# Conditioning weights requested between the output-projection loads on one queue, and one burst's transposes issued after the next burst

## The chip, the cores and the metric

The kernel runs on one core of a Trainium2 chip. The metric is the device time of one execution in microseconds (us). Engines are named as the profile names them: PE is the matrix engine (PEld its weight loads), DVE the vector engine, ACT the scalar engine, POOL the GpSimd engine, SP the sync engine. SP and POOL issue DMAs here, each on a queue of its own (q1 and q0 in the profile).

## The reference, cut to what matters

A decoder layer runs on 320 tokens: 256 of a prompt and 8 samples of 8 tokens. Every weight is shared. A conditioning vector per sequence makes six modulation vectors; the two last of them (`sc2`/`sh2` for the second norm, `g2` for the second residual) are used behind the mixing part:

```python
mod = jax.nn.silu(c) @ w_ada + b_ada
sh1, sc1, g1, sh2, sc2, g2 = [m[:, None, :] for m in jnp.split(mod, 6, axis=-1)]
...
merged = jax.nn.sigmoid(ga) * y_a + jax.nn.sigmoid(gb) * y_b
x = x + g1 * (merged @ w_o)

h2 = _rmsnorm(x, norm2_g) * (1 + sc2) + sh2
gate, up = jnp.split(h2 @ w_gu, 2, axis=-1)
x = x + g2 * ((jax.nn.silu(gate) * up) @ w_down)
```

`D_MODEL` is 2048, so `w_ada` is 2048 x 12288, `w_o` 2048 x 2048, `w_gu` 2048 x 11264, all float32.

## The kernel before, in words

Activations lie with channels on the 128 partitions and the 320 tokens along the free axis. Each float32 weight is split into a high and a low part of a shorter type (`whi` by ACT at L151, `wlo` by DVE at L152), each activation likewise, and a product is three matmuls (L165, L166, L167). A projection (`proj`, L169) takes 256 output columns at a time. It reads its weight in *chunks* of 512 rows x 256 columns (0.5 MB, one DMA on SP at L143, buffer `raw` with three slots), splits each chunk in two halves of two row blocks (`whi` and `wlo` have four slots), and gives 24 matmuls for each chunk (four row blocks, two column blocks, three products).

The output projection `w_o` is eight such units of four chunks (loop at L979), 32 chunks in all; this text counts them from 0 to 31, so that chunk `4*ui + c//4` is the one that `between(c - k0)` (L180) follows. `between` is `x1_rows` (L970), which at a unit's first chunk asks on SP for two 160 KB blocks of the saved residual stream (L975). After each unit `residual` and `sq_acc` update the residual stream and the sum of squares on DVE and ACT, and POOL makes `xs` (L985).

Beside this, `mod` is computed in *bursts* (`BURSTS`, L245): a burst multiplies 4 or 8 row blocks of `w_ada` (1024 columns wide) on PE, in four column strips at once (`ada_burst`, L273, matmuls at L284). Its weights lie in `araw`, are listed by `ada_load` (L262), and are requested piece by piece by `ada_piece` (L254) on POOL's queue. When the last burst of a column range is done, ACT copies the sums (`adasb`, L291), PE transposes them twice (L293, recorded as L129) and DVE adds the bias into `mod` (L296); this part is called the closing here.

Bursts 0 to 23 are loaded and run earlier. Bursts 24 and 25 (eight row blocks each; together the first half of `g2`) and burst 26 (four row blocks; the first quarter of the second half) are listed at L977 and requested during `w_o`: after each of the two POOL operations at L985 of a unit, one piece of two row blocks (1 MB), so ten pieces in all. They run right behind `w_o`: burst 24, the matmul that sums the squares over the partitions (`rstd_bcast`, L991), burst 25 with its closing, burst 26. Then `h2` is made (L1006 to L1015) and the gate and up projections (`w_gu`) begin, the first two side by side (`projs`, L183), their matmuls issued behind the last matmul of burst 26 (`issue_after`, L1082).

The order of each engine's instructions is set when the program is built: a planner takes the program order as priority and simulates when each instruction becomes ready. `issue_after(x)` adds that an instruction stands behind `x` in its engine's order. Each engine and each queue then works strictly in that order. Pools that are closed (`mix` and `acx`, L944 and L945) give their memory to the pools opened behind them, among them `aw` (L949), which holds `xs`, `araw` and `adasb` for bursts 24 to 26.

Of the kernel before, what the change touches and what calls it, by code (L numbers as in the profile page):

```python
# [15 lines left out]
ALU = mybir.AluOpType  # L16
# [4 lines left out]
P = 128  # L21
TP, NB, LS = 256, 8, 8
TS = NB * LS
T = TP + TS
# [58 lines left out]
def body(tc, A):  # L83
    nc = tc.nc
# [12 lines left out]
    def nm(s):  # L97
        uid[0] += 1
        return "%s_%d" % (s, uid[0])

    def misc():
        return pmisc.tile([P, 512], F32, tag="m", name=nm("pm"))

    V, S, G, PE = nc.vector, nc.scalar, nc.gpsimd, nc.tensor
# [22 lines left out]
    def tr(out, in_):  # L127
        k = in_.shape[0]
        PE.transpose(out, in_, ident[:k, :k])  # L129
# [3 lines left out]
    last_raw = []  # L133
# [35 lines left out]
    def proj(w, col, k0, k1, xh, xl, between=None):  # L169

        ps = pmain.tile([P, 2, 512], F32, tag="pm", name=nm("ps"))
        for c0 in range(k0, k1, 4):
            nk = min(4, k1 - c0)
            for j, whi, wlo in split_chunk(w[:, c0:c0 + nk, col:col + 256], nk, 256):
                kt = c0 + j
                for i in range(2):
                    mm3(ps[:, i, :T], whi[:, i * P:(i + 1) * P], wlo[:, i * P:(i + 1) * P],
                        xh[kt], xl[kt], kt == k0, kt == k1 - 1)
            if between:
                between(c0 - k0)  # L180
        return ps
# [26 lines left out]
    wada = A["w_ada"][0].rearrange("(kt p) n -> p kt n", p=P)  # L208
# [35 lines left out]
    NBA = 8  # L244
# [5 lines left out]
    ada_want = []  # L250
# [2 lines left out]

    def ada_piece(after=None):  # L254

        n, t, r = ada_want.pop(0)
        sec, b, k0, nk = BURSTS[n]
        col = (sec * KT + b) * P
        with tc.issue_after(after) if after is not None else nullcontext():
            nc.gpsimd.dma_start(t[:, r:r + 2], wada[:, k0 + r:k0 + r + 2, col:col + NBA * P])  # L260

    def ada_load(n, bufs):  # L262

        if n < len(BURSTS) and n not in ada_raw:
            nk = BURSTS[n][3]
            t = ada_raw[n] = apool[0].tile([P, nk, NBA * P], F32, tag="big" if nk == 4 else "big2", bufs=bufs if nk == 8 else 1, name=nm("araw"))
            ada_want.extend((n, t, r) for r in range(0, nk, 2))

    def ada_all():
        while ada_want:  # L270
            ada_piece()

    def ada_burst():  # L273

        n = len(ada_done)
        sec, b, k0, nk = BURSTS[n]
        ada_done.append(n)
        if k0 == 0:
            ada_ps[:] = [misc()]
        ps = ada_ps[0]  # L280
        with tc.high_priority(), tc.issue_after(last_mm[0]):
            for r in range(nk):
                for j in range(4):
                    last_ada[:] = [PE.matmul(ps[32 * j:32 * j + 32, 0:2 * P], lhsT=scT[:, k0 + r, :],  # L284
                                             rhs=ada_raw[n][:, r, 2 * j * P:(2 * j + 2) * P],
                                             start=k0 + r == 0, stop=k0 + r == KT - 1, tile_position=(0, 32 * j)).ins]
        if k0 + nk < KT:
            return
        pt = misc()
        sb = apool[0].tile([P, 2 * P], F32, tag="adasb", name=nm("adasb"))  # L290
        S.copy(sb, ps[:, 0:2 * P])  # L291
        for q in range(2):
            tr(pt[:, q * P:(q + 1) * P], sb[:, q * P:(q + 1) * P])  # L293
        blk = slice(sec * KT + b, sec * KT + b + NBA)
        bb = bada[:, blk].rearrange("p (j q) -> p j q", q=2).unsqueeze(3).broadcast_to([P, 4, 2, 9])
        V.tensor_tensor(mod[:, blk, :].rearrange("p (j q) r -> p j q r", q=2),  # L296
                        pt[:, 0:2 * P].rearrange("p (q j r) -> p j q r", q=2, j=4)[:, :, :, 0:9], bb, op=ALU.add)
        if sec == 4:
            V.tensor_tensor(mod[:, blk, :], mod[:, blk, :],
                            N2G[:, b:b + NBA].unsqueeze(2).broadcast_to([P, NBA, 9]), op=ALU.mult)  # L300
# [4 lines left out]
    def mods(sec, kt):  # L305
        return mod[:, sec * KT + kt, 1:9].unsqueeze(2).broadcast_to([P, NB, LS])

    def s3(ap):
        return ap.rearrange("p (b t) -> p b t", t=LS)
# [87 lines left out]
    with tc.tile_pool(name="head", bufs=1) as xp:  # L397
# [43 lines left out]
        for i in range(3):  # L441
            n = P if i < 2 else TS
# [469 lines left out]
    RATE = 10  # L912
    BURST_UNITS = (0, 1, 2, 3, 7, 8, 9, 10)
    ada_load(0, 1)
    ada_all()
    for h in range(1, H):
        pump(RATE)
        g = new_group(h)
        for ui, (kind, i, col) in enumerate(units(h)):
            if kind == "og" and i == 0:  # L920
                pump(len(queue))
                new_gates(g)
            ps = proj(win, col, 0, KT, hh, hl)
            evac(ps, g, kind, i, None)
            if kind == "u":
                pump(len(queue))
                st, E = gla_steps(g)
                pst, psy = pool_steps(g)
                queue += pst + st
            if ui in BURST_UNITS:  # L930
                ada_burst()
                if len(ada_done) < AMIX:
                    ada_load(len(ada_done), 1)
                    ada_all()
            pump(RATE)
        queue += psy + [merge_step(g, E)]
# [13 lines left out]
    x1 = [fp.tile([P, T], F32, name="x1_%d" % k) for k in range(KT)]  # L950
    acc = fp.tile([P, T], F32, tag="acc", name="acc1")

    def sq_acc(acc, k, first):
        if first:
            S.activation(acc, x1[k], AF.Square)
        else:
            sq = fp.tile([P, T], F32, tag="sq", bufs=2, name=nm("sq"))
            S.activation(sq, x1[k], AF.Square)
            V.tensor_tensor(acc, acc, sq, op=ALU.add)

    def residual(ps, i, k, sec):
        V.scalar_tensor_tensor(x1[k][:, 0:TP], ps[:, i, 0:TP], modp(sec, k), x1[k][:, 0:TP],
                               op0=ALU.mult, op1=ALU.add)
        t = fp.tile([P, TS], F32, tag="rt", bufs=2, name=nm("rt"))
        V.tensor_tensor(s3(t), s3(ps[:, i, TP:T]), mods(sec, k), op=ALU.mult)
        V.tensor_tensor(x1[k][:, TP:T], x1[k][:, TP:T], t, op=ALU.add)

    xs = apool[0].tile([P, KT, TS], F32, name="xs")
    tiny = fp.tile([P, 1], F32, name="tiny")
    def x1_rows(c):  # L970

        if c == 0:
            with tc.issue_after(last_raw[0]):
                for k in (2 * ui, 2 * ui + 1):
                    nc.sync.dma_start(x1[k], xspill[k])  # L975

    for n in range(AMIX, AMIX + 3):  # L977
        ada_load(n, 2)
    for ui in range(8):  # L979
        ps = proj(wo, 256 * ui, 0, KT, mh, ml, between=x1_rows)  # L980
        for i in range(2):
            residual(ps, i, 2 * ui + i, 2)
            k = 2 * ui + i
            sq_acc(acc, k, k == 0)
            gi = G.tensor_tensor(s3(xs[:, k]), s3(x1[k][:, TP:T]), mods(4, k), op=ALU.mult).ins  # L985
            if ada_want:
                ada_piece(gi)
        if ui == 6:
            S.activation(tiny, epst, AF.Sqrt)

    def rstd_bcast(acc):  # L991
        pt = misc()
        last_mm[:] = [PE.matmul(pt[:, 0:T], lhsT=ones, rhs=acc, start=True, stop=True).ins]
        rs = fp.tile([P, T], F32, tag="rs", name=nm("rs"))
        S.activation(rs, pt[:, 0:T], AF.Sqrt, scale=1.0 / D, bias=epst)
        V.reciprocal(rs, rs)
        return rs

    more[:] = [fa, None]
    ada_burst()  # L1000
    rs = rstd_bcast(acc)
    ada_burst()
    ada_burst()
    h2h = [hp.tile([P, T], F32R, tag="hh%d" % k, name="h2h%d" % k) for k in range(KT)]
    h2l = [hp.tile([P, T], F32R, tag="hl%d" % k, name="h2l%d" % k) for k in range(KT)]
    for k in range(KT):  # L1006
        t = apool[0].tile([P, T], F32, tag="h2", bufs=3, name=nm("h2"))
# [69 lines left out]
    for pi, (f0, f1) in enumerate(parts):  # L1077
# [37 lines left out]
        for ui in range(8):  # L1115
            if pi == 1 and ui == 7:
                break
            ps = proj(wdn, 256 * ui, f0, f1, ah, al)
            for i in range(2):
                k = 2 * ui + i  # L1120
# [7 lines left out]
    ps = pmain.tile([P, 2, 512], F32, tag="pm", name=nm("ps"))  # L1128
# [3 lines left out]
    for c0 in range(f0, f1, 4):  # L1132
        nk = min(4, f1 - c0)
        raw = raw_chunk(wdn[:, c0:c0 + nk, 256 * 7:256 * 8], nk, 256)
        for j in range(0, nk, 2):
            q = c0 - f0 + j
# [14 lines left out]
    with tc.manual_schedule(engines={mybir.EngineType.PE}):  # L1151
        for kt in range(f0, f1):
            PE.matmul(pb, lhsT=ahl[kt], rhs=whl[kt][0], start=kt == f0, stop=False)
            PE.matmul(pb, lhsT=ahl[kt], rhs=whl[kt][1], start=False, stop=kt == f1 - 1)
            if kt in (f0 + 7, f0 + 10):
                i = 0 if kt == f0 + 7 else 1
                k = KT - 2 + i
# [9 lines left out]
    for i in range(2):  # L1167
        k = KT - 2 + i
        t = fp.tile([P, TS], F32, tag="rt", bufs=2, name=nm("rt"))
# [26 lines left out]
```

## Time and profile before

| | us |
|---|---|
| median of three runs | 1974.52 |
| lowest, highest | 1974.08, 1975.68 |
| the profiled execution: its own time | 1972.61 |
| the profiled execution: its span | 1970.7 |
| busy PE / DVE / ACT / POOL in the span | 1927.2 / 1003.3 / 822.3 / 204.7 |

The span is the time between the first and the last recorded instruction; about 1.9 us of the execution lie outside it. The busy share of PE counts overlapping matmuls and their modelled ends, so small gaps are seen better from the start times of single matmuls in the timeline. In a timeline row stand the start, the duration (from the first to the last of the merged instructions), the engine, the line, what is written and read, the count, and in brackets how long the engine had been idle and what released it. In the view by stretches each row has the stretch, its length, the busy time and count of each engine, the granted clock, the share of the DMA engines and GB/s.

The stage of `w_o` runs from about 880 to 1006 us of the span, and the change lies between 911 and 1018 us.

### The profile page before, as it was taken

The page shows a single profiled execution, that of the slowest core. Times are in us where ns is not written, and L with a number is a line of the kernel's source. Part 1 is how long each engine was busy: PE and PEld are TensorE (multiplying, and loading weights), DVE is VectorE, ACT ScalarE, POOL GpSimd, SP SyncE. Part 2 cuts the span into 40 slices and gives each one's busy share as a digit, 9 for nine tenths or more (in the row PEclk, how much of TensorE's full clock was granted, in tenths as well). Part 3 has the DMA queues.
Part 4 walks back from the last instruction along what each step waited for, and adds up shares of the span by engine and source line. Part 5 has one row for each costly group of instructions (what it writes and reads, how often), then busy time and mean ns, then how long its engine had stood idle before and what let it go on. Part 6 is the DMA issues. An engine that isn't in the chain of part 4 may idle for free.

```text
span 1970.7 us, 34879 instructions
## 1 busy us (share of the span) xinstructions
PE 1927.2 (98%) x13900; PEld 1811.9 (92%) x13900; DVE 1003.3 (51%) x1894; ACT 822.3 (42%) x1472; POOL 204.7 (10%) x352
## 2 busy tenths in 40 slices
PE   5999999999999999999999999999999999999998
PEld 3778988988899889988989999999999999999998
DVE  2655655655356535665474444444444444444554
ACT  3323553643345433553344333433333434344444
POOL 1002211221122112111130000000000000000000
PEclk9999999999999999999999999999999999999999
DMA  9995558758865787479935554444444444444443
GB/s 339 340 338 181 189 174 292 246 192 312 279 218 168 267 292 261 129 254 326 320 114 194 191 184 142 149 153 144 157 146 152 149 152 150 150 148 149 140 150 107
DMA packets 310206, 400.95 MB, mean 203 GB/s; under 512 B 12898, under 2 KB 273858, under 8 KB 309706
## 3 DMA queue, kind: packets, MB, share of 16 engines
q1 hardware_dynamic: 279914, 291.17, 45.8%
q0 software_dynamic: 30128, 107.55, 14.8%
q8 instruction: 109, 1.79, 0.4%
q14 instruction: 55, 0.44, 0.1%
HBM read 374.23 MB, written 24.67 MB: 202 GB/s over the span
## 4 chain that ended last, share of the span: by engine, by line
PE 82%; DMA 2%; ACT 1%; DVE 1%; issue 0%; POOL 0%; ACTq 0%; DVEq 0%; POOLq 0%
PE ps L167 25%; PE ps L165 25%; PE ps L166 25%; PE pm L284 3%; PE pm L129 1%; DMA araw<-w_ada 1%; PE pm L779 1%; PE pm L758 1%; DMA raw<-w_o 1%; PE pm L723 1%; DMA raw<-w_in 1%; PE pm L712 0%; DVE wlo L152 0%; PE pm L653 0%; ACT whi L151 0%
## 5 line engine op out<-in xcount | busy, mean ns | idle before, releaser
L152 DVE TENSOR_TENSOR wlo<-raw,whi 128x512 fp32r<-128x512 f32 x941 | 648.9, 694 | 773.6 <-ACT whi L151 760.7
L151 ACT CAST whi<-raw 128x512 fp32r<-128x512 f32 x941 | 579.2, 621 | 899.9 <-PE ps L166 802.2
L165 PE MATMUL ps<-hh,whi 128*128 128x320 f32 x1408 | 441.8, 314 | 3.1 <-ACT whi L151 2.1
L167 PE MATMUL ps<-hh,wlo 128*128 128x320 f32 x1408 | 436.0, 312 | 2.0 <-DVE wlo L152 1.9
L166 PE MATMUL ps<-hl,whi 128*128 128x320 f32 x1408 | 436.4, 310 | 0.0
L165 PE MATMUL ps<-h2h,whi 128*128 128x320 f32 x1408 | 434.6, 309 | 0.0
L166 PE MATMUL ps<-h2l,whi 128*128 128x320 f32 x1408 | 434.3, 309 | 0.0
L167 PE MATMUL ps<-h2h,wlo 128*128 128x320 f32 x1408 | 434.2, 309 | 0.0
L165 PEld LDWEIGHTS ps<-hh,whi 128*128 128x128 f32 x1408 | 264.5, 188 | 27.6 <-issue 16.1
L167 PEld LDWEIGHTS ps<-hh,wlo 128*128 128x128 f32 x1408 | 263.7, 188 | 17.5 <-issue 9.5
L166 PEld LDWEIGHTS ps<-hl,whi 128*128 128x128 f32 x1408 | 264.7, 188 | 4.3 <-issue 3.2
L165 PEld LDWEIGHTS ps<-h2h,whi 128*128 128x128 f32 x1408 | 264.5, 188 | 1.2 <-ACT ah L315 1.2
L166 PEld LDWEIGHTS ps<-h2l,whi 128*128 128x128 f32 x1408 | 264.5, 188 | 0.0
L167 PEld LDWEIGHTS ps<-h2h,wlo 128*128 128x128 f32 x1408 | 264.5, 188 | 0.0
L166 PE MATMUL ps<-al,whi 128*128 128x320 f32 (+1 forms) x668 | 206.3, 309 | 0.0
L167 PE MATMUL ps<-ah,wlo 128*128 128x320 f32 (+1 forms) x668 | 205.7, 308 | 0.0
L165 PE MATMUL ps<-ah,whi 128*128 128x320 f32 (+1 forms) x668 | 205.7, 308 | 0.0
L166 PEld LDWEIGHTS ps<-al,whi 128*128 128x128 f32 x668 | 125.2, 187 | 0.1
L167 PEld LDWEIGHTS ps<-ah,wlo 128*128 128x128 f32 x668 | 125.2, 187 | 0.0
L165 PEld LDWEIGHTS ps<-ah,whi 128*128 128x128 f32 x668 | 125.2, 187 | 0.0
L165 PE MATMUL ps<-mh,whi 128*128 128x320 f32 x256 | 80.3, 314 | 3.3 <-ACT whi L151 2.6
L260 POOL DMA_DIRECT2D araw<-w_ada x64 | 45.7, 718 | 355.6 <-PE pm L284 341.0
(316 smaller groups left out, 1698.5 us busy)
## 6 DMA issues: line engine op xcount, KB each, us to landing
raw<-w_gu SPq DMA_DIRECT2D x176, 512.0 KB, 3.4
raw<-w_in SPq DMA_DIRECT2D x173, 512.0 KB, 3.9
araw<-w_ada POOLq DMA_DIRECT2D x64, 1024.0 KB, 8.0
raw<-w_down SPq DMA_DIRECT2D x80, 512.0 KB, 3.4
raw<-w_ada SPq DMA_DIRECT2D x64, 512.0 KB, 6.3
S<-state_gla POOLq DMA_DIRECT2D x16, 1024.0 KB, 8.8
o_gs<-S POOLq DMA_DIRECT2D x16, 1024.0 KB, 6.1
raw<-w_o SPq DMA_DIRECT2D x32, 512.0 KB, 7.3
```

What stands on the lines that cost most here:

```text
L129: PE.transpose(out, in_, ident[:k, :k])
L151: S.copy(hi, raw)
L152: V.tensor_sub(lo, raw, hi.bitcast(F32))
L165: PE.matmul(ps, lhsT=whi, rhs=xhi, start=start, stop=False)
L166: PE.matmul(ps, lhsT=whi, rhs=xlo, start=False, stop=False)
L167: last_mm[:] = [PE.matmul(ps, lhsT=wlo, rhs=xhi, start=False, stop=stop).ins]
L260: nc.gpsimd.dma_start(t[:, r:r + 2], wada[:, k0 + r:k0 + r + 2, col:col + NBA * P])
L284: last_ada[:] = [PE.matmul(ps[32 * j:32 * j + 32, 0:2 * P], lhsT=scT[:, k0 + r, :], rhs=ada_raw[n][:, r, 2 * j * P:(2 * j + 2) * P], start ...
L723: PE.matmul(pt, lhsT=E["kdn"][:, s, d * P:(d + 1) * P], rhs=E["vn"][:, s], start=s == 0, stop=s == 1)
L758: PE.matmul(pt[32 * j:32 * j + 32, :], lhsT=qeP[:, d, 4 * gg + j, :], rhs=E["S0", gg, d][:, j], start=False, stop=d == 0, tile_position=(0 ...
L779: PE.matmul(pt, lhsT=E["kpn"][:, j, d * P:(d + 1) * P], rhs=E["vp"][:, gg], start=True, stop=True)
```

## The change

The pieces of bursts 24, 25 and 26 become one row block each (`nr` is 1: 0.5 MB, twenty pieces). They are requested on SP instead of POOL, one behind each `w_o` chunk from chunk 11 on (`x1_rows`), issued behind that chunk's own load. POOL no longer issues pieces behind its `xs` operations. All other bursts keep pieces of two row blocks on POOL. The closing of burst 25 becomes a function of its own, `ada_close`, and is called after burst 26 instead of before it.

```diff
     def ada_piece(after=None):
 
-        n, t, r = ada_want.pop(0)
+        n, t, r, nr = ada_want.pop(0)
         sec, b, k0, nk = BURSTS[n]
         col = (sec * KT + b) * P
         with tc.issue_after(after) if after is not None else nullcontext():
-            nc.gpsimd.dma_start(t[:, r:r + 2], wada[:, k0 + r:k0 + r + 2, col:col + NBA * P])
-
-    def ada_load(n, bufs):
+            q = nc.sync if after is not None else nc.gpsimd
+            q.dma_start(t[:, r:r + nr], wada[:, k0 + r:k0 + r + nr, col:col + NBA * P])
+
+    def ada_load(n, bufs, nr=2):
...
-            ada_want.extend((n, t, r) for r in range(0, nk, 2))
+            ada_want.extend((n, t, r, nr) for r in range(0, nk, nr))
...
-    def ada_burst():
+    def ada_burst(later=False):
...
         if k0 + nk < KT:
             return
+        if later:
+            return lambda: ada_close(sec, b, ps)
+        ada_close(sec, b, ps)
+
+    def ada_close(sec, b, ps):
+
         pt = misc()
         sb = apool[0].tile([P, 2 * P], F32, tag="adasb", name=nm("adasb"))
         S.copy(sb, ps[:, 0:2 * P])
...
                 for k in (2 * ui, 2 * ui + 1):
                     nc.sync.dma_start(x1[k], xspill[k])
+        if 4 * ui + c // 4 >= 11 and ada_want:
+            ada_piece(last_raw[0])
 
     for n in range(AMIX, AMIX + 3):
-        ada_load(n, 2)
+        ada_load(n, 2, 1)
...
-            gi = G.tensor_tensor(s3(xs[:, k]), s3(x1[k][:, TP:T]), mods(4, k), op=ALU.mult).ins
-            if ada_want:
-                ada_piece(gi)
+            G.tensor_tensor(s3(xs[:, k]), s3(x1[k][:, TP:T]), mods(4, k), op=ALU.mult)
...
     ada_burst()
     rs = rstd_bcast(acc)
+    close = ada_burst(True)
     ada_burst()
-    ada_burst()
+    close()
```

## The prediction

> **What bounds the kernel now.** I read the page first, for the busy times. Then the view by stretches over the stage that the change touches, and in it the timeline of PE.
>
> ```profile
> PE 1927.2 (98%) x13900; PEld 1811.9 (92%) x13900; DVE 1003.3 (51%) x1894; ACT 822.3 (42%) x1472; POOL 204.7 (10%) x352
> 940.00:949.00 9.00, 6.10 (x36) 5.05 (x35) 3.02 (x6) 2.28 (x4) 0.00 (x0) 1.00 1.05 379
> 949.20:952.50 3.30, 3.30 (x14) 3.30 (x14) 2.79 (x8) 2.52 (x5) 2.02 (x4) 0.50 0.83 235
> 953.00:1003.00 50.00, 50.00 (x343) 50.00 (x342) 26.17 (x54) 19.91 (x35) 4.72 (x8) 1.00 0.75 256
> 1003.00:1018.00 15.00, 13.16 (x185) 8.12 (x184) 11.31 (x25) 5.89 (x15) 5.16 (x13) 1.00 0.23 73
> ```
>
> PE is busy 98% of the span, so the kernel is bound by PE, and a change can only win where PE waits or runs slowly. Two places in the stretches that the change touches do so. From 940 to 949 us PE is busy for 6.10 of 9 us, and right behind it stands a stretch at a granted clock of 0.50. From 1003 to 1018 us PE is busy for 13.16 of 15 us. Between them (953 to 1003) it is full: there is nothing to win.
>
> The first place, in the timeline of PE:
>
> ```profile
> 940.21 0.31 PE L167 MATMUL ps<-mh,wlo 128*128 128x320 f32 x1
> 940.81 0.41 PE L165 MATMUL ps<-mh,whi 128*128 128x320 f32 x1 [0.30 <-ACT whi L151]
> 941.79 0.31 PE L165 MATMUL ps<-mh,whi 128*128 128x320 f32 x1
> 944.73 0.31 PE L167 MATMUL ps<-mh,wlo 128*128 128x320 f32 x1
> 947.30 0.41 PE L165 MATMUL ps<-mh,whi 128*128 128x320 f32 x1 [2.26 <-ACT whi L151]
> 948.02 0.41 PE L167 MATMUL ps<-mh,wlo 128*128 128x320 f32 x1 [0.17 <-DVE wlo L152]
> 952.60 0.31 PE L166 MATMUL ps<-ml,whi 128*128 128x320 f32 x1
> 1005.55 0.31 PE L167 MATMUL ps<-mh,wlo 128*128 128x320 f32 x1
> ```
>
> A chunk is 24 matmuls. 941.79 is the fourth and 944.73 the last of chunk 15, 20 steps apart: 0.147 us each, 3.52 us per chunk. Without waits the fourth would have come at 940.21 + 4 x 0.147 = 940.80: 0.99 us lost. Chunk 16 should begin at 944.88; 952.60 is its 23rd matmul (22 steps behind its first), due at 948.11: 4.49 us lost, of which 2.4 us are the idle time before 947.30 and the rest the wait before 948.02 and matmuls at half the clock. Together 5.5 us. A second count agrees: chunks 15 to 31 are 408 matmuls; without loss the last would start at 940.36 + 407 x 0.1466 = 1000.0, and it starts at 1005.55.
>
> Why the weights came late, from the DMA view of 923 to 940 us, the chain of waits and the timelines of POOL and SP:
>
> ```profile
> q0 software_dynamic: 1146, 4.44, 67.2%
> q1 hardware_dynamic: 1220, 1.22, 21.6%
> araw<-w_ada POOLq DMA_DIRECT2D x6, 1024.0 KB, 12.7
> raw<-w_o SPq DMA_DIRECT2D x4, 512.0 KB, 14.8
> 924.17 0.76 POOL L260 DMA_DIRECT2D araw<-w_ada  x1
> 933.56 0.76 POOL L260 DMA_DIRECT2D araw<-w_ada  x1
> 931.76 14.77 DMA raw<-w_o
> 923.73 0.40 POOL L985 TENSOR_TENSOR xs<-x,mod 128x64 f32<-128x64 f32 x1 [16.85 <-PE pm L129]
> 919.31 5.08 SPq L143 DMA_DIRECT2D raw<-w_o  x2
> ```
>
> POOL's first `xs` operation waited 16.85 us for the transposes of burst 23 (the pool's memory was not free), and then six pieces of 1 MB went out from 924.17 to 933.56. Over those 17 us POOL's queue got 4.44 MB and SP's 1.22 MB, and the load of chunk 16, issued at 931.76, landed 14.77 us later.
>
> **The change part by part.** *Pieces on SP, one behind each chunk's load.* The bytes are the same (20 x 0.5 MB for 10 x 1 MB); only their order changes. A w_o load now has at most the pieces before it on its own queue in front of it, in place of up to 6 MB that share the engines with it. Is the queue fast enough?
>
> ```profile
> DMA packets 40886, 48.28 MB, mean 345 GB/s; under 512 B 1773, under 2 KB 36018, under 8 KB 40642
> raw<-w_ada SPq DMA_DIRECT2D x61, 512.0 KB, 6.4
> raw<-w_gu SPq DMA_DIRECT2D x176, 512.0 KB, 3.4
> 975.44 0.37 SPq L143 DMA_DIRECT2D raw<-w_o  x1
> L151 ACT CAST whi<-raw 128x512 fp32r<-128x512 f32 x941 | 579.2, 621 | 899.9 <-PE ps L166 802.2
> L152 DVE TENSOR_TENSOR wlo<-raw,whi 128x512 fp32r<-128x512 f32 x941 | 648.9, 694 | 773.6 <-ACT whi L151 760.7
> 1007.85 0.55 POOL L985 TENSOR_TENSOR xs<-x,mod 128x64 f32<-128x64 f32 x2 [13.52 <-DVE x L966]
> ```
>
> In the head of the kernel (5 to 145 us) the core moved 345 GB/s, two thirds of it in the 61 loads of 512 KB on SP that the next row shows. A slot of one chunk now asks for 524 KB of w_o, 524 KB of w_ada and a quarter of a unit's 328 KB of residual rows: 1.13 MB in 3.52 us, 321 GB/s, 93% of that rate. The slack of a w_o load, from chunk 27: issued at 975.44, landed 3.4 us later (the undisturbed landing of w_gu loads), cast and subtracted by 980.2 (0.62 and 0.69 us); its matmuls begin five chunks before 1005.70, at 988.1. That is 7.9 us of slack, and a piece ahead takes 0.524 MB / 345 GB/s = 1.5 us of it.
>
> The start needs its own look. The pieces write into the same pool as `xs`, so I take them to be free at the same time, about 923.7. By then SP has issued chunk 13 and stands before chunk 14 (the second of the two at 919.31, so at 924.0). The planner, which simulates this, should put pieces 0, 1 and 2 there, at once. Chunk 14 then has three pieces before it: 2.1 MB, 6.1 us, landed at about 932 with 1.9 us of fixed time (3.4 less 1.5); it must be there by 935.5 (1.3 us before 936.84, where chunk 14 starts). It fits, and every later chunk has one or two pieces before it. So I take all of the 5.5 us. Bounds: 5.5 won, or a new stall of the same size.
>
> What else moves. SP: 20 more issues of 0.38 us, 7.6 us over some 70; a w_o load comes at most 0.4 us later at a time, inside its slack; the residual rows behind a piece have a unit (14 us) before they are read. The last piece follows chunk 30 and is read a burst later, some 20 us. POOL: ten issues of 0.76 us go; nothing waits for POOL there, since the last `xs` is ready at 1008.40, before PE has summed the squares that h2 needs (burst 25, which follows that sum, starts at 1010.18, below). Both: nothing. Without that slack on SP each issue would cost its 0.38 us.
>
> *The closing of burst 25 behind burst 26.* Timelines of PE, ACT and DVE:
>
> ```profile
> 1010.18 3.66 PE L284 MATMUL pm<-araw,scT 128*32 128x256 f32 x64
> 1015.68 0.33 PE L129 MATMUL pm<-cst,adasb 128*128 128x128 f32 x1 [1.84 <-ACT adasb L291]
> 1015.94 1.93 PE L284 MATMUL pm<-araw,scT 128*32 128x256 f32 x32
> 1017.80 0.33 PE L129 MATMUL pm<-cst,adasb 128*128 128x128 f32 x1
> 1017.88 0.39 PE L165 MATMUL ps<-h2h,whi 128*128 128x320 f32 x1
> 1015.11 0.24 ACT L1012 CAST h2h<-h 128x64 fp32r<-128x64 f32 x1 [0.57 <-POOL h L1010]
> 1015.26 0.37 ACT L291 COPY adasb<-pm 128x256 f32<-128x256 f32 x1
> 1015.38 0.23 DVE L1015 TENSOR_TENSOR h2l<-h,h2h 128x64 fp32r<-128x64 f32 x1
> ```
>
> Burst 25 ends at 1013.84; its sums are copied by ACT only at 1015.26, behind the first casts of h2; so PE idles 1.84 us, transposes, and runs burst 26 only then. With the closing behind it burst 26 fills the gap: 1013.84 + 1.86 = 1015.70. The copy is done at 1015.63 and the two transposes follow (0.26 + 0.08 us, as now), so the first w_gu matmul comes at about 1016.05 instead of 1017.88. What is late next is h2: its first block is complete at 1015.35 (high part) and 1015.61 (low part), in time by 0.4 us. So 1.8 us, if what w_gu reads next keeps up:
>
> ```profile
> 1022.00:1036.00 14.00, 14.00 (x97) 14.00 (x96) 14.00 (x35) 9.59 (x25) 8.43 (x14) 1.00 0.36 114
> 1024.50 0.78 DVE L152 TENSOR_TENSOR wlo<-raw,whi 128x512 fp32r<-128x512 f32 x1
> ```
>
> DVE is full there, with h2 and the splits of w_gu. The tightest split ends at 1025.28; it is the sixth half chunk, which PE reaches at 1017.88 + 5 x 1.76 = 1026.68 and whose `wlo` is first read 0.29 us later: 1.69 us early. With PE 1.8 us ahead that becomes 0.1 us late. So I take 1.7 us; bounds 0 (DVE holds everything) and 2.2 us (w_gu starts at 1015.70 with the transposes somewhere behind).
>
> The sum: 5.5 + 1.7 = 7.2 us off the profiled execution's 1972.61, which gives 1965.4. That execution was 1.9 us below the median of the three runs, 1974.52; against the median the forecast is **1967.3 us**, 0.36% less. About 0.2% (3.9 us) is what a measurement of this kernel can tell from no change.
>
> **The rivals.** *1. SP waits where POOL waited.* If piece 0 stands right behind chunk 11, it holds SP until 923.7, and chunks 12 and 13 with it:
>
> ```profile
> 908.75 6.68 SPq L143 DMA_DIRECT2D raw<-w_o  x3
> ```
>
> Chunks 10, 11 and 12 are these three, so chunk 12 went out at 915.06 and would go at 924.1. With one piece before it (3.0 us for both, 1.9 fixed) it lands at about 929.0 and is split at 930.3, against matmuls at 929.8: about 0.5 us lost, and 1.7 more if the clock falls to half for one stretch of 3.3 us again. That gives 1967.8 to 1969.5. For it: the wait of 16.85 us. Against it: the planner sees the same wait. Chance 0.13.
>
> *2. The tail stays.* PE is held by the copy or by DVE as before, so only the 5.5 us are won: 1969.0. For it: DVE without a gap. Chance 0.08.
>
> *3. The pieces come in a crowd all the same,* so the change doesn't do what it says. If the planner takes the memory to be free later, it collects the pieces of all chunks issued so far. The slack of 7.9 us holds five pieces (7.6 us). Six to eight before one w_o load lose 1.2 to 4.3 us, and 1.7 us by the clock: 1970.2 to 1973.3. Against it: at 924.0 only three are due. Chance 0.09.
>
> *4. Slower: the one queue does not carry both.* If loads on SP ran one after the other, each slot would take 2 x 3.4 = 6.8 us instead of 3.52: over 20 slots 66 us, less 8 us of slack, so 1967.3 + 58 = 2025 us. Short of that, the point from which it is slower by 0.2% is a stall of 7.2 + 3.9 = 11.1 us, a slot of 3.52 + (11.1 + 7.9)/20 = 4.47 us: 253 GB/s. Against it stand the 345 GB/s of the head. Chance 0.06. [...]
>
> **How the numbers follow.** The forecast has 0.64, the rivals 0.13, 0.08, 0.09 and 0.06. The range reaches from 1964.8 (the tail at its upper bound, and the 1.9 us between executions) to 1971.5 (rivals 1 and 2 and the mild end of 3); what lies above is rival 4 and the worse part of 3, about 0.12, with some 0.05 for what I haven't seen. Faster by over 0.2% (below 1970.6) are the forecast and rivals 1 and 2, less 0.03 for their spread: 0.82; within 0.2%: 0.12; slower 0.06.
>
> **What would show it.** On SP a piece behind each w_o load from about 924 us on; landings of w_o near 5 us in place of 14.8; no idle time of PE over 0.3 us and no half clock between 930 and 1003; the last w_o matmul near 1000.0; burst 26 directly behind burst 25, and the first w_gu matmul some 10.5 us behind the last of w_o (now 12.3). It is wrong if w_o loads still land over 8 us late, if SP waits more than 5 us before the first piece, or if DVE's `wlo` holds PE behind the start of w_gu.

## The result and the profile after

The changed kernel takes 1965.56 us (median of six runs, 1963.26 to 1967.86) against 1974.30 us before (six runs, 1973.08 to 1975.93). The ratio is 0.9958 with a 95% interval of 0.9947 to 0.9968: 8.3 us faster, 6.3 to 10.5. The profiled execution of after has a span of 1964.4 us, 6.3 us less than that of before. The added lines shift line numbers: L260 is now L261, L284 is L285, L291 is L298, L975 is L982, L985 is L994, L993 is L1000.

The view by stretches of the changed kernel, in the columns of the prediction:

```profile
923.00:940.00 17.00, 17.00 (x118) 16.99 (x117) 9.05 (x19) 6.21 (x11) 1.72 (x6) 1.00 0.87 308
940.00:949.00 9.00, 9.00 (x64) 9.00 (x63) 5.34 (x13) 4.04 (x8) 0.55 (x2) 1.00 1.03 361
949.20:952.50 3.30, 3.30 (x24) 3.30 (x23) 1.60 (x3) 1.02 (x3) 0.00 (x0) 1.00 1.03 359
1000.00:1016.00 16.00, 16.00 (x206) 12.35 (x205) 12.79 (x29) 7.04 (x20) 6.70 (x18) 1.00 0.21 68
1015.50:1029.50 14.00, 14.00 (x97) 13.85 (x96) 14.00 (x35) 10.19 (x27) 9.14 (x18) 1.00 0.28 90
```

From 940 to 949 us PE is busy for all 9 us (6.10 before), the clock stays at 1.00 where it was 0.50, and from 1000 to 1016 us PE has no gap. Both places that the prediction named are gone. The last row begins as far behind the first w_gu matmul (4.1 us) as the row from 1022 us in the prediction: DVE is full there as before.

SP's timeline, its waits and its landings from 920 to 985 us (minimum, median and longest time from issue to landing, first of the w_o loads, then of the pieces):

```profile
920.59 0.38 SPq L143 DMA_DIRECT2D raw<-w_o  x1
924.92 1.28 SPq L261 DMA_DIRECT2D araw<-w_ada  x3
926.31 0.65 SPq L143 DMA_DIRECT2D raw<-w_o  x1
927.00 0.58 SPq L261 DMA_DIRECT2D araw<-w_ada  x1
928.99 0.38 SPq L143 DMA_DIRECT2D raw<-w_o  x1
929.42 0.72 SPq L261 DMA_DIRECT2D araw<-w_ada  x1
SPq L261 <- PE pm L129: 3.6, 1, 3.6
DMA to landing us min/median/max: 3.7/5.9/8.2
DMA to landing us min/median/max: 4.8/6.8/8.7
```

SP stands before the first piece for 3.6 us, because of the transposes that POOL had waited for; the planner put three pieces there, before chunk 14, and from then on one behind each chunk. The w_o loads, at most 8.2 us on their way, no longer make PE wait.

PE between the last w_o matmul and the start of w_gu:

```profile
1001.34 0.31 PE L167 MATMUL ps<-mh,wlo 128*128 128x320 f32 x1
1001.58 3.66 PE L285 MATMUL pm<-araw,scT 128*32 128x256 f32 x64
1005.24 0.81 PE L1000 MATMUL pm<-acc,cst 128*128 128x320 f32 x2
1005.98 5.46 PE L285 MATMUL pm<-araw,scT 128*32 128x256 f32 x96
1011.36 0.57 PE L165 MATMUL ps<-h2h,whi 128*128 128x320 f32 x2
1015.00 0.38 PE L129 MATMUL pm<-cst,adasb 128*128 128x128 f32 x2
```

Bursts 25 and 26 are one row now (96 matmuls), w_gu follows at once, and the transposes come among its matmuls, 3.6 us behind the first.

The time goes at these places. The first w_o matmul comes at 880.7 us (879.7 before; nothing ahead of it was changed), the last at 1001.34: 120.7 us for the stage against 125.9. The tail to the first w_gu matmul takes 10.0 us against 12.3. The rest, behind that, takes 953.0 against 952.8. Together: +1.0 - 5.2 - 2.3 + 0.2 = -6.3 us, the difference of the spans.

### The profile page after: what moved, and what is told of

It is laid out like the page before. It is cut to its first block, busy times and chain, and to the rows that moved or that the text cites. A ratio compares the mean times of both kernels' runs of the same rounds, so it can differ in the third digit from the quotient of the medians.

```text
span 1964.4 us, 34887 instructions
## 1 busy us (share of the span) xinstructions
PE 1924.6 (98%) x13900; PEld 1812.0 (92%) x13900; DVE 1004.3 (51%) x1894; ACT 823.6 (42%) x1472; POOL 192.8 (10%) x342
## 3 DMA queue, kind: packets, MB, share of 16 engines
q8 instruction: 109, 1.79, 0.4%
## 4 chain that ended last, share of the span: by engine, by line
PE 84%; DMA 1%; ACT 1%; DVE 1%; issue 0%; ACTq 0%; DVEq 0%
PE ps L167 25%; PE ps L165 25%; PE ps L166 25%; PE pm L285 3%; PE pm L129 1%; PE pm L765 1%; PE pm L786 1%; PE pm L730 1%; DMA raw<-w_in 1%; DMA araw<-w_ada 0%; PE pm L719 0%; DVE wlo L152 0%; PE pm L660 0%; PE psy L165 0%; ACT whi L151 0%
## 5 line engine op out<-in xcount | busy, mean ns | idle before, releaser
L166 PE MATMUL ps<-ml,whi 128*128 128x320 f32 x256 | 79.2, 309 | 0.0
```

The lines of the kernel that those rows point to most:

```text
L166: PE.matmul(ps, lhsT=whi, rhs=xlo, start=False, stop=False)
```

## The experiments

Each kernel was timed beside the kernel before, on the same chip. The two stage times come from each profile in the same way: the w_o stage from its first to its last matmul, the tail from there to the first w_gu matmul.

| | first w_o matmul at, us | w_o stage, us | tail, us | ratio to before (95%) |
|---|---|---|---|---|
| before | 879.7 | 125.9 | 12.3 | |
| the change | 880.7 | 120.7 | 10.0 | 0.9958 (0.9947 to 0.9968) |
| e7, the change again | 881.3 | 120.9 | 10.0 | 0.9957 (0.9944 to 0.9971) |
| e1, SP part alone | 882.2 | 120.9 | 12.3 | 0.9979 (0.9970 to 0.9988) |
| e2, closing alone | 881.7 | 124.5 | 10.0 | 0.9988 (0.9979 to 0.9997) |
| e3, POOL from unit 2 | 880.4 | 121.1 | 13.8 | 0.9976 (0.9967 to 0.9986) |
| e8, POOL from unit 1 | 882.4 | 121.8 | 12.3 | 0.9981 (0.9971 to 0.9990) |
| e5, SP with 1 MB pieces | 882.1 | 120.4 | 12.3 | 0.9973 (0.9963 to 0.9983) |
| e4, eight pieces at once on SP | 881.7 | 124.8 | 14.0 | 1.0001 (0.9991 to 1.0011) |
| e6, the copy first on ACT | 882.6 | 124.3 | 11.0 | 0.9991 (0.9982 to 1.0000) |

The first column is a part that no kernel here changes, and it spreads over 2.9 us. So the spans of single executions are no measure of a few microseconds; the stage times are, and the ratios of many runs.

**e1: the SP part alone.**

```diff
-    close = ada_burst(True)
     ada_burst()
-    close()
+    ada_burst()
```

> The twenty pieces on SP as in the change, the closing of burst 25 where it was before. Theory (the two parts are independent, the first removes a stall of 5.5 us): 5.5 us faster than before (5.0 to 6.0); in the profile the w_o stage takes 120.7 us from its first to its last matmul (125.9 before), and the 1.84 us of idle time of PE before the transposes stay. Rival (the pieces on SP are worth more than the stall shows, since the medians of the whole change differ by 8.7 us): 7 us or more.

Measured: 4.1 us faster (2.4 to 5.9), stage 120.9 us, tail 12.3 us. The stage is within 0.2 us of what the theory said and the idle time before the transposes stays (timeline of PE):

```profile
1007.81 3.66 PE L285 MATMUL pm<-araw,scT 128*32 128x256 f32 x64
1013.30 0.33 PE L129 MATMUL pm<-cst,adasb 128*128 128x128 f32 x1 [1.84 <-ACT adasb L298]
1013.56 1.93 PE L285 MATMUL pm<-araw,scT 128*32 128x256 f32 x32
```

The gain of the whole execution lies below the theory's 5.0 to 6.0 us, but its interval reaches into them. The rival's 7 us lies outside the interval.

**e2: the closing alone.** The pieces as in the kernel before, on POOL; of the diff only `ada_close` and

```diff
+    close = ada_burst(True)
     ada_burst()
-    ada_burst()
+    close()
```

> Only the closing of burst 25 is moved behind burst 26; the pieces stay on POOL with 1 MB each. Theory: 2.0 us faster than before (1.5 to 2.5): from the last w_o matmul to the first of w_gu 10.0 us in place of 12.3, of which the transposes take back 0.3 later; the stall of chunk 16 and the half clock behind it stay. Rival (DVE, full with h2 and the splits, sets the pace of w_gu's start): under 0.5 us faster, with PE waiting for wlo between 1018 and 1036 us.

Measured: 2.4 us faster (0.6 to 4.1), tail 10.0 us; the stall and the half clock are there (stage 124.5 us). Between 1018 and 1036 us PE's weight loads wait for `wlo` once, for 0.17 us; DVE, full there as before, does not set the pace, and the rival falls. The two parts act on different places, as the profile of before showed them.

**e7: the change again.**

> The changed kernel itself, timed again. Theory (the profile's stages hold the whole gain: 5.2 and 2.3 us less 0.2): 7.3 us faster than before, 0.9963. Rival (the medians of the first runs hold more than the stages show): 8.7 us, 0.9956 or less.

Measured: 0.9957 (0.9944 to 0.9971), 8.5 us with an interval that holds both 7.3 and 8.7. Inconclusive on that question; the stages (120.9 and 10.0 us) repeat.

**e3: POOL's queue kept, the crowd taken away.**

```diff
-            if ada_want:
+            if ui >= 2 and ada_want:
                 ada_piece(gi)
```

> The kernel before, but the ten 1 MB pieces on POOL's queue begin at unit 2 in place of unit 0: two behind each unit from the third to the seventh, so never six in a crowd; same queue, same size, same tail. Theory A (the crowd of six is what made the load of chunk 16 late): 5 to 5.5 us faster than before, no idle time of PE over 0.3 us in the w_o stage, w_o loads land within 10 us. Theory B (it is the sharing of the engines with POOL's queue, whose packets are larger, that makes w_o late, whatever the pace): a stall behind each pair of pieces, under 2 us faster or slower than before.

Measured: 4.7 us faster (2.8 to 6.5). The w_o stage takes 121.1 us, on POOL's queue with 1 MB pieces, two at a time. In the stage PE waits only for two other things, by the view of its waits (waiter, what it waited for, us in total, times, longest):

```profile
PE pm L284 <- DMA araw<-w_ada: 1.0, 1, 1.0
PE ps L165 <- DVE mg L885: 0.8, 1, 0.8
```

The longest landing of a w_o load was 10.3 us, a little over the 10 expected. Theory A holds: it was the crowd, and neither the queue nor the size. But the tail became 1.5 us longer, which I had not expected. The timelines of POOL, ACT, DVE and PE show why:

```profile
991.82 0.76 POOL L260 DMA_DIRECT2D araw<-w_ada  x1
1000.91 2.18 ACT L151 CAST whi<-raw 128x512 fp32r<-128x512 f32 x4 [5.61 <-DMA raw<-w_gu]
1001.56 1.90 DVE L152 TENSOR_TENSOR wlo<-raw,whi 128x512 fp32r<-128x512 f32 x3 [5.54 <-ACT whi L151]
1003.38 0.48 DVE L962 SCALAR_TENSOR_TENSOR x<-ps,mod,x 128x256 f32<-128x256 f32 x1
1006.92 0.81 PE L993 MATMUL pm<-acc,cst 128*128 128x320 f32 x2 [1.50 <-DVE acc L959]
```

The pieces that start later also end later, the last at 991.82. They meet the first w_gu loads, one of which, issued at 991.7, takes 9.1 us to land (3.4 undisturbed), so that its casts on ACT come only at 1000.91; their three splits stand ahead of the last residual in DVE's order, so the sum of squares is late and PE waits 1.50 us for it. In the changed kernel the last piece goes out at 982.27.

**e8: a crowd of four on POOL.** As e3, with `ui >= 1`.

> The kernel before, but the ten 1 MB pieces on POOL's queue begin at unit 1 in place of unit 0: two when the pool's memory is free, two some 8 us later, then two per unit up to the sixth. A crowd of four in 10 us in place of six. Theory (what counts is how many bytes go ahead of chunk 16's load, against its slack): that load lands about 5 us earlier than the 14.8 us of before, inside its slack: no idle time of PE over 0.5 us in the w_o stage, which takes 121 to 121.5 us; and since the last pieces go out one unit earlier than with the start at unit 2, PE does not wait before the matmul that sums the squares: 12.3 us from the last w_o matmul to the first of w_gu (13.9 with the start at unit 2). Rival (six pieces are not special, four also stall): over 123 us.

Measured: 3.8 us faster (2.0 to 5.7), stage 121.8 us, tail 12.3 us. PE waits 0.5 us for a w_o cast and 0.3 us for `wlo` in the stage, and its w_o loads take up to 12.0 us (15.7 before, 8.2 with the change), at the edge of their slack. That longest one is chunk 16's, which landed 2.8 us earlier than before and not 5. The stage came out 0.3 us above what I expected. So six pieces of 1 MB in 10 us stall PE for over 2 us, four for half a microsecond, two not at all; and the pieces ending a unit earlier give the tail of before.

**e5: 1 MB pieces on SP.** As e1, one piece of two row blocks behind every second chunk.

```diff
-        if 4 * ui + c // 4 >= 11 and ada_want:
+        if 4 * ui + c // 4 >= 11 and (c // 4) % 2 and ada_want:
...
-        ada_load(n, 2, 1)
+        ada_load(n, 2)
```

> As the run with only the SP part of the change, but ten pieces of two row blocks (1 MB), one behind every second chunk from chunk 11 on, on SP. Theory (the size of a piece does not matter as long as at most two or three stand before a w_o load): the w_o stage takes 120.6 to 121.2 us as with 0.5 MB pieces, w_o loads land within 9 us. Rival (the halving matters): a w_o load behind a 1 MB piece comes too late, the stage is over 122 us.

Measured: 5.3 us faster (3.4 to 7.3), stage 120.4 us. The longest landing of a w_o load was 9.3 us, a little over the 9 expected, and PE did not notice it. Halving the pieces is worth nothing that shows here.

**e4: a crowd on SP.** As e1, with

```diff
+        m = 4 * ui + c // 4
-        if 4 * ui + c // 4 >= 11 and ada_want:
-            ada_piece(last_raw[0])
+        for _ in range(8 if m == 15 else 1):
+            if m >= 15 and ada_want:
+                ada_piece(last_raw[0])
```

> As the run with only the SP part of the change, but no piece until chunk 15, then eight pieces (4.2 MB) at once behind it on SP, then one behind each chunk. Theory (a crowd delays w_o on any queue; on one queue by the bytes ahead at about 345 GB/s): the load of chunk 16 is issued some 4 us behind the eight pieces, still has about 3.5 MB (10 us) before it and lands 12 to 14 us after its issue; its slack is about 7.4 us, so PE idles 2 to 4 us before chunk 16, and half a clock behind it may cost 1.7 more: the w_o stage takes 123 to 126 us from first to last matmul (121.0 without the crowd). Rival (one queue serves in order, so that a crowd there does no harm): 121 us, no idle time of PE over 0.3 us.

Measured: no gain left (1.0001, 0.9991 to 1.0011), stage 124.8 us. The timelines of SP and PE, the landings of w_o from 920 to 990 us, and the stretch behind the stall:

```profile
931.00 4.00 SPq L261 DMA_DIRECT2D araw<-w_ada  x8
935.59 0.38 SPq L143 DMA_DIRECT2D raw<-w_o  x1
948.57 0.53 PE L165 MATMUL ps<-mh,whi 128*128 128x320 f32 x1 [1.95 <-ACT whi L151]
DMA to landing us min/median/max: 3.5/6.7/12.2
950.00:952.00 2.00, 2.00 (x9) 2.00 (x9) 0.74 (x2) 0.42 (x1) 0.00 (x0) 0.50 1.05 373
```

Chunk 16's load goes out behind the eight pieces and takes 12.2 us to land; PE idles 1.95 us before it, a little under the 2 to 4 expected, and then runs at half the clock. So one queue is no protection; the spacing is. The tail, which this kernel has as before, took 14.0 us instead of 12.3, of which more below.

**e6: the copy first on ACT.** The kernel before, with the casts of h2 behind the copy of burst 25's sums:

```diff
-        S.copy(sb, ps[:, 0:2 * P])
+        last_copy[:] = [S.copy(sb, ps[:, 0:2 * P]).ins]
...
-        S.activation(h2h[k][:, 0:TP], t[:, 0:TP], AF.Identity, bias=modp(3, k))
-        S.copy(h2h[k][:, TP:T], t[:, TP:T])
+        with tc.issue_after(last_copy[0]):
+            S.activation(h2h[k][:, 0:TP], t[:, 0:TP], AF.Identity, bias=modp(3, k))
+            S.copy(h2h[k][:, TP:T], t[:, TP:T])
```

> The kernel before, with the casts of h2 on ACT put behind the copy of burst 25's sums, so that the copy comes first; closing and pieces as before. Theory (PE's 1.84 us before the transposes are the copy's place in ACT's order): the copy starts at once when burst 25 is done, the idle time falls to 0.4 to 0.5 us, and from the last w_o matmul to the first of w_gu it takes 10.9 to 11.2 us in place of 12.3: about 1.3 us of the 2.0 us that moving the closing gives. Rival (h2's first block sets the start): the casts that now wait hold the first w_gu matmul, 12 us or more.

Measured: 1.8 us faster (0.0 to 3.6), tail 11.0 us. The timelines of ACT and PE:

```profile
1015.25 0.37 ACT L292 COPY adasb<-pm 128x256 f32<-128x256 f32 x1 [3.09 <-PE pm L285]
1011.52 3.66 PE L285 MATMUL pm<-araw,scT 128*32 128x256 f32 x64
1015.67 0.33 PE L129 MATMUL pm<-cst,adasb 128*128 128x128 f32 x1 [0.49 <-ACT adasb L292]
```

Burst 25 ends at 1011.52 + 3.66 = 1015.18, the copy starts 0.07 us later, and the idle time is 0.49 us in place of 1.84. So the gap was the copy's place in ACT's order. Putting burst 26 into the gap gives more (10.0 us), since it also hides the copy itself, and the transposes (0.34 us) no longer stand ahead of w_gu.

## Why the prediction was right

*The w_o stage.* The term was 5.5 us. From the end of burst 21, ahead of the change (the matmul behind it at 905.08 before and 906.37 after), to the last w_o matmul (1005.55 and 1001.34), the profile shows 5.50 us less. That the count of matmuls came out exact is in part luck. In it lay the half clock behind the stall, and this is not sure to be there: in e6 PE idled 2.23 us at the same place, and no half clock followed. In it lay also 0.99 us lost at chunk 15, which e2 didn't lose. With the pieces as before, the stage took 124.5 us in e2 and 124.3 in e6, so the term was right for the execution that it was read from; for another it could have been 1.5 us less.

*The start on SP.* The prediction put pieces 0, 1 and 2 before chunk 14, free when the transposes of burst 23 are done. That is what SP's rows show. Rival 1 (SP held behind chunk 11) did not come: the wait moved to SP, 3.6 us long, at a place where the next w_o load was not yet due. Rival 4 fell too: SP carried both, 361 GB/s from 940 to 949 us where 321 were asked for. One sign that the prediction gave for being wrong, w_o loads over 8 us, came by 0.2 us without any wait of PE: it was set too tight against a slack of 7.9 us on top of 3.4.

*The crowd.* Rival 3 is shown as a danger by e4. Its arithmetic (pieces times 1.5 us against a slack of 7.9 us) would have had eight pieces lose 4.3 us and 1.7 by the clock. It measured 1.95 us of idle time and a further 1.9 (124.8 - 120.9 - 1.95), most of it by the clock (3.41 us at a granted clock of 0.50 from 948.70 us on). That some pieces had moved by the time that chunk 16's load was issued, as the expectation of e4 had it, is the likely reason for the smaller stall.

*The tail.* The term was 1.7 us, between 0 and 2.2; it measured 2.3, of which 0.2 come back behind it: 2.1 us. The step that was mis-sized is the place of the transposes. The prediction let the first w_gu matmul wait for the copy and both transposes (0.34 us); the planner put the copy at 1013.21 and the transposes at 1015.00, behind the first w_gu matmuls. What the prediction said of DVE held. DVE stays full, and the split of the sixth half chunk, which was to hold PE by 0.1 us, holds PE's weight loads by 0.15 us. That the size is so near is in part luck, since the order of DVE's work changed (timelines of DVE and of the weight loads, changed kernel):

```profile
1020.40 0.68 DVE L152 TENSOR_TENSOR wlo<-raw,whi 128x512 fp32r<-128x512 f32 x1
1021.14 0.19 PEld L167 LDWEIGHTS ps<-h2h,wlo 128*128 128x128 f32 x1 [0.15 <-DVE wlo L152]
```

The prediction listed a wait for `wlo` behind the start of w_gu as a sign of being wrong, though its own sum had one of 0.1 us in it; it came with about that size. The same wait stands in e2 and e7 (0.17 us each), at the same half chunk. In e1, which has the closing where it was, there is none.

*The rest.* The measured 1965.56 us lie in the range, 1964.8 to 1971.5. By the stages of this profile the forecast of 7.2 us is right (5.2 + 2.3 - 0.2 = 7.3 us, with 0.3 us of the w_o term lost to a longer wait of burst 21 for its weights). The ratios give 8.3 and 8.5 us with intervals that hold 7.3; the two parts alone (e1 and e2) give 4.1 + 2.4 = 6.5 us. Whether a microsecond more is real stays open. A candidate is the half clock: of the six profiled executions with the 1.84 us gap in the tail one (e4) paid it. An estimate from the windows described below, if the gap can begin anywhere in a window: it lies whole in one window of 3.41 us in (3.41 - 1.84) / 3.41 = 46% of the cases and then costs 1.7 us (e4, 3.61 less 1.93), 0.8 us on average. That was not tried.

## What to carry to other kernels

A transfer that nobody waits for can still cost time when its pieces are released together: what counted here is how many bytes stand before a load that is needed, against that load's slack (PE idled 2.26 us behind six pieces of 1 MB, 0.5 us behind four, not at all behind two). Space them, as the change and e3 did on either queue (stage 120.7 and 121.1 us against 125.9), and let the last go out before the next stage's first loads (a tail of 12.3 us in e1 and e8, 13.8 in e3). Where an engine idles for another's turn in the middle of a chain, a job that needs no result of it can be moved into the gap, and here this gave more than hurrying the other engine (10.0 against 11.0 us).

## What the runs showed of the hardware

**A gap of 2 us can cost as much again, or nothing.** The stretches behind the same gaps, by kernel. First e4, the idle time of 1.84 us in the tail:

```profile
1016.67 0.33 PE L129 MATMUL pm<-cst,adasb 128*128 128x128 f32 x1 [1.84 <-ACT adasb L298]
1016.93 3.61 PE L285 MATMUL pm<-araw,scT 128*32 128x256 f32 x32
1018.00:1020.00 2.00, 2.00 (x26) 0.81 (x16) 1.65 (x4) 1.18 (x5) 1.84 (x5) 0.50 0.00 0
```

Then e6, the stall before chunk 16:

```profile
949.51 0.41 PE L165 MATMUL ps<-mh,whi 128*128 128x320 f32 x1 [2.23 <-ACT whi L151]
950.00:953.00 3.00, 2.83 (x20) 2.76 (x20) 2.60 (x9) 1.00 (x3) 0.94 (x2) 1.00 1.06 333
```

In e4 burst 26 took 3.61 us instead of 1.93, at a granted clock of 0.50, behind a gap of 1.84 us; before, e1, e3, e5 and e8 have the same gap and no half clock. In e6 the clock stayed at 1.00 behind 2.23 us; before, e2 and e4 had half the clock behind 2.26, 2.26 and 1.95 us. So the length alone does not decide.

What tells the cases apart can be read from the traces. In each of the ten, the granted clock changes only at instants that lie a whole number of 3.413 us apart (in e4 the half clock begins at 948.70 and at 1016.97, 20 times 3.413 us apart). Counted from the first instruction, they lie at other places in each run: near 949 us there is one at 949.08 before, at 948.06 with the change, at 948.70 in e4 and at 948.78 in e6. Cut at these instants, the view by stretches gives for e4, for e6 and for the kernel before:

```profile
1013.56:1016.97 3.41, 1.57 (x29) 0.70 (x23) 3.31 (x8) 1.84 (x6) 2.83 (x7) 1.00 0.00 0
1016.97:1020.38 3.41, 3.41 (x33) 1.38 (x32) 2.68 (x8) 2.41 (x9) 2.93 (x8) 0.50 0.02 5
945.37:948.78 3.41, 1.91 (x14) 1.64 (x12) 0.00 (x0) 0.00 (x0) 0.00 (x0) 1.00 1.02 391
948.78:952.19 3.41, 2.51 (x15) 2.25 (x16) 2.61 (x8) 1.33 (x3) 0.13 (x1) 1.00 1.09 352
1013.93:1017.34 3.41, 1.66 (x29) 1.03 (x33) 3.35 (x10) 2.47 (x9) 3.17 (x9) 1.00 0.02 5
1017.34:1020.75 3.41, 3.41 (x32) 3.00 (x25) 3.41 (x11) 2.11 (x7) 2.61 (x7) 1.00 0.00 0
```

In e4 the gap of 1.84 us lies whole in one window, and the next window runs at half the clock. In e6 an instant cuts the 2.23 us in two, PE is idle for 1.50 and 0.90 us in the two windows, and the clock stays at 1.00. In the kernel before, 0.09 us of the 1.84 fall outside the window, and the clock stays too. From where the records of the clock begin (27 to 37 us) to the end, the ten traces hold 24 windows at full clock with 1.79 us or more of PE idle, and each was followed by a window at half the clock (before: 1.79 us in the window from 945.67 us, 2.59 us in that from 1962.84); after the other windows at full clock, with 1.75 us or less, none came. One place ahead of the change shows the same: at about 245 us every kernel has gaps of 1.3 and 0.8 us close together, and e1, e2, e6 and e8, where 1.88 us or more of them fell into one window, ran the next at half the clock; in the other six it was 1.49 us at most, and the clock stayed. So part of the spread in the first column of the table comes from this.

**Two queues side by side moved nearly the same number of packets.** In the crowd of before, from 923 to 940 us, POOL's queue moved 1146 packets and SP's 1220, but 4.44 MB against 1.22 MB, since POOL's packets are about four times as large (3.9 KB against 1.0 KB on average, from the two rows in the prediction). So SP's queue, with rows of 1 KB, got about a fifth of the bytes (1.22 of 5.66 MB) while six pieces with rows of 4 KB were on their way on POOL's beside it. e3 and e8 show how much this matters: PE does not wait for a w_o load with two pieces of 1 MB at a time on POOL's queue (e3), and 0.5 us with four (e8).
